# The last feed-forward block's products seven instead of eight, and the table load of attention tied to eight silus

## The chip, the cores and the metric

One NeuronCore of a Trainium2 chip runs the whole program. The metric is the device time of one execution in microseconds; lower is better.

## The reference

Two layers over x of 512 tokens by 1024 features, float32. Each layer is: a half-step SwiGLU block, a mixer, another half-step SwiGLU block, each with an RMS norm before it, and a final RMS norm:

```
x = x + 0.5 * (silu(h @ w_gate) * (h @ w_up)) @ w_down      h = rms_norm(x, gain), hidden width 2816
layer 0 mixer: 4 heads of differential attention (softmax) and 4 heads of stick-breaking attention
layer 1 mixer: gated DeltaNet, 8 heads
out = rms_norm(x, final_norm)
```

Stick-breaking attention needs for each score z the logarithm of a sigmoid, a reverse running sum over the keys and an exponential: for each block of scores an Abs, an Exp, a Ln and one more Exp on ScalarE.

## The kernel before

x lies in SBUF with features on the partitions: eight chunks of 128 features by 512 tokens (`self.x`). All large products are float32 made from two parts, a rounded high part and the rest (`split_to`, L225 and L226 for operands, L173 and L174 for weights in `panel`), and three matmuls each: high by high, high by low, low by high (`mm3`, L180 to L182). The matmuls that carry the work are therefore 128 x 128 by 512 or 256 columns.

A feed-forward block (`ffn`) cuts the 22 tiles of the hidden width into groups. In three of the four blocks the groups have 6, 8 and 8 tiles. The first group's gate and up products are made by `eight`: for a pair of hidden tiles 2 weight matrices x 2 tiles x 8 feature chunks x 3 = 96 matmuls of 512 columns. The other two groups use `seven`: tokens and features are halved and the 2 x 2 block product is formed from seven half-size products with sums and differences of the operands, for a pair 7 x 2 x 4 x 3 = 168 matmuls of 256 columns (L499). The combined x operands are prepared once a block by `quarters`; the combined weights are loaded and partly summed by accumulating DMAs that GpSimd issues (L472), by two sums on VectorE (L513, L525), and split as other weights are. After each group `add_out` multiplies the group's hidden tiles with their rows of w_down and adds the result to x by VectorE (L374).

The fourth block, the last of the program, has groups of 12 and 10 tiles, all by `eight`. After its first group x is turned to tokens on the partitions (`to_tokens`, L546 and L549: 32 transposes, eight copies), and `add_tok` adds both groups' results token-wise. In its last call each 128 tokens' row goes on into `finish`, the final norm: squares on ScalarE, a power on GpSimd, two scalings and one output DMA for 128 tokens by 1024 features (L601). In the last half of the output columns the last three weight panels are multiplied together token block by token block, so that the four blocks end one after the other.

Every activation needs its function in ScalarE's active table. At the start of attention, `exp_ln_tables` (L187) puts in a load of the one set `natural_log_exp_and_others`; an ordering tie to `self.last_act`, the silu issued last in program order, says that it comes after that silu, and attention's first Exp (L626) is tied behind the load. Loads that the program does not name are put in by the build where a function is not in the active set; the profile shows them under the line of the activation they serve.

The order of instructions on each engine is chosen when the program is built, from the program order, data dependencies, buffers and such ties. PSUM tiles come from three rings: `mm_ps` with two buffers, `a_ps` and `b_ps` with three each. In stick-breaking attention (`sb_block`) three blocks of scores are live at once (`W_SB`), two heads by four query blocks a group, and two groups follow each other; the next group's projections and the first part of the output projection are multiplied between them.

Of the kernel before, what the change touches and what calls it, by code (L numbers as in the profile page):

```python
# [10 lines left out]
F32 = mybir.dt.float32  # L11
F32R = mybir.dt.float32r
AF = mybir.ActivationFunctionType
ALU = mybir.AluOpType

P = 128
T = 512
D = 1024
KC = D // P
FF = 2816  # L20
NF = FF // P
NB = T // P
# [78 lines left out]
class Trunk:  # L101
# [4 lines left out]
    def __init__(self, ctx, tc):  # L106
        self.tc = tc
        self.nc = tc.nc
        self.const = ctx.enter_context(tc.tile_pool(name="const", bufs=1))
        self.xp = ctx.enter_context(tc.tile_pool(name="xp", bufs=1))  # L110
        self.wp = ctx.enter_context(tc.tile_pool(name="wp", bufs=4))
        self.np_ = ctx.enter_context(tc.tile_pool(name="np", bufs=2))
        self.ps = ctx.enter_context(tc.tile_pool(name="ps", bufs=2, space=bass.MemoryType.PSUM))
        self.dram = ctx.enter_context(tc.tile_pool(name="dr", bufs=1, space=bass.MemoryType.DRAM))
        self.ahead, self.pending, self.pin = [], [], None
        self.te = self.nc.tensor
        self.x = [self.xp.tile([P, T], F32, name=f"x{c}") for c in range(KC)]
        self.consts()
# [65 lines left out]
    def exp_ln_tables(self):  # L184

        nc = self.nc
        ld = nc.scalar.add_instruction(mybir.InstLoadActFuncSet(  # L187
            name=nc.get_next_instruction_name(), act_func_set_id=EXP_LN_SET, ins=[], outs=[]))
        dep = mybir.DependencyInfo(mybir.DependencyClass.NoSync, mybir.DependencyReason.DATA)
        self.tc.add_manual_dep(ld.ins, self.last_act.ins.name, dep, reason="tables")  # L190
        return ld, dep


# [184 lines left out]
    def ffn(self, wg, wu, wd, first=False, last=None):  # L378

        nc = self.nc
        sizes, ring = ((12, 10), 14) if last is not None else ((6, 8, 8), 10)
        with ExitStack() as st:
            pool = st.enter_context(self.tc.tile_pool(name="ffn", bufs=2))
            f0 = 0
            for size in sizes:
                hid = []
                for f in range(f0, f0 + size, 2):
                    if f0 and last is None:  # L390
                        inner = self.seven(pool, wg, wu, f)
                    else:
                        inner = self.eight(pool, wg, wu, f, first)
                    for j, hd in enumerate(inner):
                        slot = (f + j) % ring
                        both = pool.tile([P, 2 * T], F32R, tag=f"hid{slot}", name=f"hid{slot}",
                                         bufs=1)
                        h, l = both[:, :T], both[:, T:]
                        self.split_to(h, l, hd)
                        hid.append((h, l))  # L400
                if f0 == 0:
                    if last is None:
                        self.quarters(pool)
                    else:
                        self.to_tokens(pool)
                if last is None:
                    self.add_out(hid, wd, f0 * P, 0.5, (self.a_ps, self.a_ps, self.b_ps, self.b_ps))
                else:
                    self.add_tok(hid, wd, f0 * P, 0.5, f0 and self.finish(pool, *last))
                f0 += size  # L410

    def small(self, pool, tag):
# [3 lines left out]
    def eight(self, pool, wg, wu, f, first):  # L416

        nc = self.nc
        g = self.proj_pair(wg, f * P, (self.a_ps, self.b_ps) if f == 2 else None,
                           2 if first and f == 0 else 1)  # L420
        u = self.proj_pair(wu, f * P, (self.a_ps, self.b_ps))
        for j in range(2):
            gr, sg, ur, hd = (self.small(pool, t) for t in ("gr", "sg", "ur", "hd"))
            nc.vector.tensor_tensor(gr, g[j], self.rb, op=ALU.mult)
            self.last_act = nc.scalar.activation(sg, gr, AF.Silu)
            nc.vector.tensor_tensor(ur, u[j], self.rb, op=ALU.mult)
            nc.vector.tensor_tensor(hd, sg, ur, op=ALU.mult)  # L427
            yield hd
# [35 lines left out]
    def seven(self, pool, wg, wu, f):  # L464
# [65 lines left out]
        for lo, hi in ((X, c21), (c12, c22)):  # L530
            sg, hd = self.small(pool, "sg"), self.small(pool, "hd")
            for i, c in enumerate((lo, hi)):
                s = slice(i * 256, (i + 1) * 256)
                self.last_act = nc.scalar.activation(sg[:, s], c[:, :256], AF.Silu)
                nc.vector.tensor_tensor(hd[:, s], sg[:, s], c[:, 256:], op=ALU.mult)
            yield hd

    def to_tokens(self, pool):
        nc = self.nc
        self.xt = []  # L540
        for b in range(NB):
            t = pool.tile([P, D], F32, name=f"xt{b}", bufs=1)
            for hf in range(2):
                ps = self.a_ps()
                for c in range(4):
                    nc.tensor.transpose(out=ps[:, c * P:(c + 1) * P],  # L546
                                        in_=self.x[hf * 4 + c][:, b * P:(b + 1) * P],
                                        identity=self.ident)
                nc.vector.tensor_copy(t[:, hf * 512:(hf + 1) * 512], ps)  # L549
            self.xt.append(t)  # L550

    def add_tok(self, parts, w, row0, factor, after=None):


        nc = self.nc
        n = len(parts)
        for dh in range(2):
            ps = [self.a_ps(), self.a_ps(), self.b_ps(), self.b_ps()]
            starts = list(range(0, n, 2))
            groups = [[f0] for f0 in starts[:-NSPL]] + [starts[-NSPL:]]  # L560
            for group in groups if dh else [[f0] for f0 in starts]:
                ws = [self.panel(w[row0 + f0 * P:row0 + (f0 + 2) * P, dh * 512:(dh + 1) * 512]
                                 .rearrange("(k p) c -> p k c", p=P), 2, 512) for f0 in group]
                for b in range(NB):
                    s = slice(b * P, (b + 1) * P)
                    for f in range(group[0], group[-1] + 2):
                        h, l = ws[(f - group[0]) // 2]
                        ph, pl = parts[f]
                        self.mm3(ps[b], (ph[:, s], pl[:, s]), (h[:, f % 2], l[:, f % 2]),
                                 f == 0, f == n - 1)  # L570
            for b in range(NB):
                xs = self.xt[b][:, dh * 512:(dh + 1) * 512]
                nc.vector.scalar_tensor_tensor(xs, ps[b], factor, xs, ALU.mult, ALU.add)
                if after:
                    after(b, dh)

    def finish(self, pool, gain, out):

        nc = self.nc
        gb = pool.tile([P, D], F32, name="gfin", bufs=1)  # L580
        nc.scalar.dma_start(gb, gain.rearrange("(o d) -> o d", o=1).broadcast_to([P, D]))
        sums = [pool.tile([P, 2], F32, name=f"fss{b}", bufs=1) for b in range(NB)]
        halves = slice(0, T), slice(T, D)

        def step(b, hf):
            x, ss = self.xt[b], sums[b]
            sq = self.np_.tile([P, T], F32, tag="sq", name="sq")
            nc.scalar.activation(sq, x[:, halves[hf]], AF.Square, accum_out=ss[:, hf:hf + 1])
            if hf == 0:
                nc.vector.tensor_scalar(ss[:, 0:1], ss[:, 0:1], 1.0 / D, EPS, ALU.mult, ALU.add)  # L590
                nc.vector.tensor_tensor(x[:, halves[0]], x[:, halves[0]], gb[:, halves[0]],
                                        op=ALU.mult)
                return
            ms = pool.tile([P, 1], F32, tag="fms", name="fms")
            nc.vector.scalar_tensor_tensor(ms, ss[:, 1:2], 1.0 / D, ss[:, 0:1], ALU.mult, ALU.add)
            r = pool.tile([P, 1], F32, tag="fr", name="fr")
            self.rpow(r, ms, 1)
            nc.scalar.activation(x[:, halves[0]], x[:, halves[0]], AF.Copy, scale=r)
            nc.vector.scalar_tensor_tensor(x[:, halves[1]], x[:, halves[1]], r, gb[:, halves[1]],
                                           ALU.mult, ALU.mult)  # L600
            nc.sync.dma_start(out[b * P:(b + 1) * P, :], x)  # L601

        return step

# [724 lines left out]
```

## Time and profile before

| what | value |
|---|---|
| median of 3 runs | 2018.27 us (2018.04 to 2020.41) |
| the profiled execution's own time | 2018.62 us |
| its span, first to last instruction | 2016.9 us |
| VectorE, ScalarE, GpSimd busy | 65%, 44%, 13% of the span |
| mean granted TensorE clock | 0.992 |
| DMA | 230.28 MB, mean 114 GB/s |

The profiled execution is 0.35 us over the median and 1.7 us longer than its own span. PE is TensorE's matmuls, PEld its weight loads, DVE VectorE, ACT ScalarE, POOL GpSimd, SP SyncE. A busy PE is modelled from starts: where matmuls follow closely the count of matmuls in a stretch is the better measure of what one costs.

### The profile page before, as it was taken

How to read it: one execution, taken by the hardware profiler on the slowest of the kernel's cores; microseconds unless marked ns; L12 is line 12 of the kernel's file. 1: busy time of each engine (PE TensorE's matmuls, PEld its weight loads, DVE VectorE, ACT ScalarE, POOL GpSimd, SP SyncE). 2: the span in 40 equal slices, each digit the busy share in tenths (PEclk: the TensorE clock that was granted, in tenths of full speed). 3: DMA queues.
4: the chain of work that ended last, by engine and by line, in shares of the span. 5: the costliest groups of instructions: out<-in, count | busy, mean ns of one | idle time of the engine just before them, and what ended most of it. 6: DMA issues, size and time to landing. Idle time of an engine off the chain costs nothing.

```text
span 2016.9 us, 29447 instructions
## 1 busy us (share of the span) xinstructions
PE 1967.6 (98%) x11514; PEld 1720.1 (85%) x11514; DVE 1304.0 (65%) x2058; ACT 897.3 (44%) x1577; POOL 254.6 (13%) x394
## 2 busy tenths in 40 slices
PE   8999999999899999999999999998899999999998
PEld 7899898888778899998889999876787788888887
DVE  6867485796557776575677667577577575443543
ACT  5434254466874344353334434455455453222322
POOL 1021110100000021110103011005441400000000
PEclk9999999999999999999999999999999999999999
DMA  7568453221135487543648654344333233322331
GB/s 200 151 132 209 92 128 105 88 83 53 47 88 136 127 171 176 114 105 106 156 131 173 167 125 95 106 116 107 80 81 86 72 110 94 95 94 94 97 101 73
DMA packets 291263, 230.28 MB, mean 114 GB/s; under 512 B 31618, under 2 KB 266420, under 8 KB 291124
## 3 DMA queue, kind: packets, MB, share of 16 engines
q1 hardware_dynamic: 209604, 195.21, 31.7%
q0 software_dynamic: 50688, 25.17, 10.2%
q10 hardware_dynamic: 30832, 8.02, 1.7%
q8 instruction: 90, 1.47, 0.3%
q14 instruction: 49, 0.40, 0.1%
HBM read 223.10 MB, written 5.26 MB: 113 GB/s over the span
## 4 chain that ended last, share of the span: by engine, by line
PE 60%; POOL 5%; DMA 2%; DVE 2%; issue 1%; ACT 1%; ACTq 0%; POOLq 0%; DVEq 0%
PE pa L499 7%; PE pa L182 5%; PE pa L180 5%; PE pa L181 5%; PE pb L182 5%; PE pb L180 5%; PE pb L181 5%; PE mm L95 5%; PE pb L499 5%; PE mm L499 5%; PE mm L181 3%; PE mm L182 3%; PE mm L180 3%; POOL tmp L1162 2%; POOL rr L1165 2%
## 5 line engine op out<-in xcount | busy, mean ns | idle before, releaser
L174 DVE TENSOR_TENSOR wl<-raw,wh 128x1024 fp32r<-128x1024 f32 (+1 forms) x252 | 295.4, 1173 | 271.6 <-ACT wh L173 270.7
L173 ACT CAST wh<-raw 128x1024 fp32r<-128x1024 f32 (+1 forms) x252 | 254.4, 1010 | 427.8 <-PE pb L181 153.5
L180 PE MATMUL mm<-xnh,wh 128*128 128x512 f32 (+1 forms) x432 | 168.7, 394 | 7.9 <-DVE qT L663 5.6
L182 PE MATMUL mm<-xnh,wl 128*128 128x512 f32 (+1 forms) x432 | 168.6, 392 | 0.0
L181 PE MATMUL mm<-xnl,wh 128*128 128x512 f32 (+1 forms) x432 | 168.2, 390 | 0.0
L226 DVE TENSOR_TENSOR wl<-raw,wh 128x1024 fp32r<-128x1024 f32 x72 | 88.0, 1223 | 79.0 <-ACT wh L225 79.0
L225 ACT CAST wh<-raw 128x1024 fp32r<-128x1024 f32 x72 | 75.5, 1049 | 113.6 <-PE pb L499 43.9
L95 PE MATMUL mm<-xnh,wh 128*128 128x512 f32 x256 | 109.1, 426 | 12.9 <-DVE cx L1051 12.9
L499 PE MATMUL pa<-sx,wh 128*128 128x256 f32 x576 | 109.9, 283 | 0.0
L180 PEld LDWEIGHTS mm<-xnh,wh 128*128 128x128 f32 x432 | 82.9, 192 | 25.5 <-DVE qT L663 6.6
L181 PE MATMUL pa<-hid,wh 128*128 128x512 f32 x264 | 102.8, 389 | 0.0
L182 PE MATMUL pa<-hid,wl 128*128 128x512 f32 x264 | 102.7, 389 | 0.0
L181 PE MATMUL pb<-hid,wh 128*128 128x512 f32 x264 | 102.7, 389 | 0.0
L182 PE MATMUL pb<-hid,wl 128*128 128x512 f32 x264 | 102.7, 389 | 0.0
L180 PE MATMUL pa<-hid,wh 128*128 128x512 f32 x264 | 102.3, 389 | 0.0
L180 PE MATMUL pb<-hid,wh 128*128 128x512 f32 x264 | 102.2, 389 | 0.0
L472 POOL DMA_DIRECT2D raw<-in_ffn_w_gate_dram x24 | 30.9, 1289 | 561.0 <-DMA raw<-in_ffn_w_gate_dram 306.8
L95 PE MATMUL mm<-xnl,wh 128*128 128x512 f32 x256 | 101.6, 397 | 0.0
L95 PE MATMUL mm<-xnh,wl 128*128 128x512 f32 x256 | 101.5, 396 | 0.0
L182 PEld LDWEIGHTS mm<-xnh,wl 128*128 128x128 f32 x432 | 82.7, 191 | 15.9 <-issue 0.5
L181 PEld LDWEIGHTS mm<-xnl,wh 128*128 128x128 f32 x432 | 82.8, 192 | 15.6 <-issue 0.2
L225 ACT CAST hid<-hd 128x512 fp32r<-128x512 f32 x88 | 54.5, 619 | 81.3 <-DVE hd L427 72.9
(395 smaller groups left out, 5626.8 us busy)
## 6 DMA issues: line engine op xcount, KB each, us to landing
raw<-in_ffn_w_down_dram SPq DMA_DIRECT2D x88, 512.0 KB, 3.7
raw<-in_ffn_w_gate_dram SPq DMA_DIRECT2D x40, 512.0 KB, 3.7
raw<-in_ffn_w_up_dram SPq DMA_DIRECT2D x40, 512.0 KB, 3.6
raw<-in_gdn_w_in_dram SPq DMA_DIRECT2D x32, 512.0 KB, 3.9
sr<-in_ffn_w_gate_dram SPq DMA_DIRECT2D x24, 512.0 KB, 3.8
sr<-in_ffn_w_up_dram SPq DMA_DIRECT2D x24, 512.0 KB, 4.9
raw<-in_att_w_in_dram SPq DMA_DIRECT2D x24, 512.0 KB, 3.6
sb<-in_ffn_w_gate_dram SPq DMA_DIRECT2D x24, 256.0 KB, 3.8
```

The costliest lines, as they stand in the source:

```text
L95: return self.tc.keep_in_program_order(self.engine.matmul(*args, **kw))
L173: nc.scalar.copy(out=h[:, :n], in_=raw[:, :n])
L174: nc.vector.tensor_tensor(l[:, :n], raw[:, :n], h[:, :n].bitcast(F32), op=ALU.subtract)
L180: self.te.matmul(out, lhsT=lh, rhs=rh, start=start, stop=False)
L181: self.te.matmul(out, lhsT=lh, rhs=rl, start=False, stop=False)
L182: self.te.matmul(out, lhsT=ll, rhs=rh, start=False, stop=stop)
L225: nc.scalar.copy(out=h, in_=src)
L226: nc.vector.tensor_tensor(l, src, h.bitcast(F32), op=ALU.subtract)
L472: eng.dma_start(v[:, q * 4:q * 4 + 4], w[kh * 512:(kh + 1) * 512, f * P + lo:f * P + hi] .rearrange("(k p) c -> p k c", p=P), **kw)
L499: nc.tensor.matmul(out, lhsT=wt[:, q * 4 + k], rhs=xt, start=start and q + k + i == 0, stop=q == 1 and k == 3 and i == 2, skip_group_check ...
L1162: nc.gpsimd.tensor_tensor(p, rr[:, :k, j:j + 1].broadcast_to(sh), lb[:, j, j + 1:].rearrange("p (o m) -> p o m", o=1) .broadcast_to(sh), o ...
L1165: nc.gpsimd.tensor_tensor(rr[:, :k, j + 1:], rr[:, :k, j + 1:], p, op=ALU.subtract)
```

## The change

Three edits. The last block gets the groups 6, 8, 8 of the others: the first group by `eight`, the other two by `seven`; `add_out` serves its first two groups, and x is turned to tokens only ahead of the last group, into the buffers of x's own chunks. The final norm uses smaller scratch buffers and writes each 128 tokens in two output DMAs. The table load of attention is tied to the last eight silus in place of one.

```diff
@@ exp_ln_tables
-        self.tc.add_manual_dep(ld.ins, self.last_act.ins.name, dep, reason="tables")
+        for act in self.silus[-8:]:
+            self.tc.add_manual_dep(ld.ins, act.ins.name, dep, reason="tables")
@@ ffn
-        sizes, ring = ((12, 10), 14) if last is not None else ((6, 8, 8), 10)
+        sizes, ring = (6, 8, 8), 10
-                    if f0 and last is None:
+                    if f0:
                         inner = self.seven(pool, wg, wu, f)
                 if f0 == 0:
-                    if last is None:
-                        self.quarters(pool)
-                    else:
-                        self.to_tokens(pool)
-                if last is None:
+                    self.quarters(pool)
+                if last is None or f0 + size < NF:
                     self.add_out(hid, wd, f0 * P, 0.5, (self.a_ps, self.a_ps, self.b_ps, self.b_ps))
                 else:
-                    self.add_tok(hid, wd, f0 * P, 0.5, f0 and self.finish(pool, *last))
+                    self.to_tokens()
+                    self.add_tok(hid, wd, f0 * P, 0.5, self.finish(pool, *last))
@@ eight, seven
-            self.last_act = nc.scalar.activation(sg, gr, AF.Silu)
+            self.silus.append(nc.scalar.activation(sg, gr, AF.Silu))
@@ to_tokens
+        self.xt = [[] for _ in range(NB)]
+        for hf, mk in enumerate(((self.b_ps, self.a_ps), (self.mm_ps, self.a_ps))):
+            ps = [mk[b // 2]() for b in range(NB)]
+            for b in range(NB):
                 for c in range(4):
+                    nc.tensor.transpose(out=ps[b][:, c * P:(c + 1) * P],
                                         in_=self.x[hf * 4 + c][:, b * P:(b + 1) * P],
                                         identity=self.ident)
+            for b in range(NB):
+                c = hf * 4 + b
+                t = self.xp.tile([P, T], F32, tag=f"x{c}", name=f"xt{c}")
+                if b % 2:
+                    nc.scalar.copy(out=t, in_=ps[b])
+                else:
+                    nc.vector.tensor_copy(t, ps[b])
+                self.xt[b].append(t)
@@ add_tok
-            ps = [self.a_ps(), self.a_ps(), self.b_ps(), self.b_ps()]
+            ps = [self.b_ps(), self.b_ps(), self.a_ps(), self.a_ps()]
@@ finish
-        gb = pool.tile([P, D], F32, name="gfin", bufs=1)
+        gb = pool.tile([P, D], F32, tag="sb", name="gfin")
...
-            nc.sync.dma_start(out[b * P:(b + 1) * P, :], x)
+            for t, s in zip(x, halves):
+                nc.sync.dma_start(out[b * P:(b + 1) * P, s], t)
```

## Rows read from the trace of the kernel before

**Rows 1.** The page's first part: busy time and share of the span.

```profile
PE 1967.6 (98%) x11514; PEld 1720.1 (85%) x11514; DVE 1304.0 (65%) x2058; ACT 897.3 (44%) x1577; POOL 254.6 (13%) x394
```

**Rows 2.** Busy by stretch (PE, PEld, DVE, ACT, POOL (count), clock, DMA): feed-forward groups.

```profile
711.30:791.95 80.65, 80.65 (x674) 80.63 (x672) 62.33 (x75) 39.28 (x53) 18.21 (x14) 1.00 0.84 183
...
1183.60:1264.24 80.64, 80.64 (x673) 80.61 (x672) 62.33 (x75) 39.28 (x53) 13.02 (x10) 1.00 0.56 119
1846.41:1955.17 108.76, 108.76 (x481) 90.09 (x480) 50.76 (x59) 32.45 (x39) 0.00 (x0) 1.00 0.34 107
```

**Rows 3.** Busy by stretch, same columns: stick-breaking batches, then differential attention.

```profile
489.00:530.00 41.00, 32.08 (x144) 24.05 (x143) 21.71 (x47) 38.88 (x63) 2.06 (x2) 0.92 0.10 33
549.00:586.00 37.00, 32.09 (x139) 24.73 (x138) 22.97 (x42) 35.22 (x62) 0.00 (x0) 0.91 0.11 36
390.00:440.00 50.00, 50.00 (x319) 45.26 (x318) 46.33 (x110) 30.49 (x74) 0.00 (x0) 1.00 0.24 75
```

**Rows 4.** ScalarE's groups by line, 488 to 592 us: busy, mean ns, idle.

```profile
L816 ACT ACT_TABLE_LOAD x14 | 18.0, 1283 | 0.2
L826 ACT ACT_TABLE_LOAD x9 | 11.5, 1283 | 0.2
...
L815 ACT ACT_TABLE_LOAD x5 | 6.4, 1283 | 0.1
```

**Rows 5.** ScalarE in order of time (start, us, instruction): three short stretches.

```profile
315.74 1.28 ACT L187 ACT_TABLE_LOAD   x1
...
318.09 1.28 ACT L534 ACT_TABLE_LOAD   x1
...
321.64 0.41 ACT L534 ACTIVATE sg<-ur 128x256 f32<-128x256 f32 x1
...
387.82 1.28 ACT L626 ACT_TABLE_LOAD   x1
...
490.73 1.28 ACT L816 ACT_TABLE_LOAD   x1
...
492.24 0.29 ACT L813 ACTIVATE e<-z 128x128 f32<-128x128 f32 x1
492.55 1.28 ACT L815 ACT_TABLE_LOAD   x1
```

**Rows 6.** TensorE's waits, 488 to 592 us: total, times, longest.

```profile
PE mm L180 <- DVE qT L663: 5.6, 1, 5.6
PE pa L832 <- ACT aT L801: 4.1, 3, 2.0
```

**Rows 7.** TensorE by line and shape, 489 to 530 us: count, busy, mean ns.

```profile
L180 PE MATMUL mm<-xnh,wh 128*128 128x512 f32 x30 | 13.8, 459 | 5.8 <-DVE qT L663 5.6
...
L808 PE MATMUL pb<-kT,qT 128*128 128x512 f32 x4 | 2.0, 593 | 0.0
...
L770 PE MATMUL pa<-v,aT 128*128 128x128 f32 x9 | 1.2, 275 | 0.0
```

**Rows 8.** The same view, 549 to 586 us.

```profile
L180 PE MATMUL mm<-xnh,wh 128*128 128x512 f32 x32 | 13.8, 437 | 1.4 <-DVE x L374 1.4
...
L832 PE MATMUL pa<-aT,v 128*128 128x128 f32 x24 | 4.1, 322 | 3.5 <-ACT aT L801 3.5
```

**Rows 9.** The chain that ended last, near 1777 us: start, us, what.

```profile
1777.60 0.87 PE pa L546 x8
```

**Rows 10.** The token tiles: each instruction's count, min/median/max ns, first and last start.

```profile
L549 DVE COPY xt<-pa x8: 678/680/691, 1778.2 to 1789.6; 128x512 f32<-128x512 f32 x8
...
L601 SPq DMA_DIRECT2D out_dram<-xt x4: 332/344/357, 2004.9 to 2013.0; - x4
```

**Rows 11.** The quartered x, same columns.

```profile
L442 DVE SCALAR_TENSOR_TENSOR xr<-x,norms,rb x24: 739/743/748, 42.6 to 991.8; 128x512 f32<-128x512 f32 x24
```

**Rows 12.** VectorE in order of time, end of another block's last seven.

```profile
1264.45 0.69 DVE L505 TENSOR_TENSOR ur<-pb,u 128x512 f32<-128x512 f32 x1 [0.31 <-PE pb L499]
```

**Rows 13.** The gate weights' loads: time from issue to landing.

```profile
DMA to landing us min/median/max: 2.8/4.4/10.0
```

More of the change, by code (lines that the diff above doesn't have):

```diff
@@ L114, in __init__ @@
         self.dram = ctx.enter_context(tc.tile_pool(name="dr", bufs=1, space=bass.MemoryType.DRAM))
-        self.ahead, self.pending, self.pin = [], [], None
+        self.ahead, self.pending, self.pin, self.silus = [], [], None, []
         self.te = self.nc.tensor
@@ L378, in ffn @@
     def ffn(self, wg, wu, wd, first=False, last=None):
-        nc = self.nc
-        sizes, ring = ((12, 10), 14) if last is not None else ((6, 8, 8), 10)
+        sizes, ring = (6, 8, 8), 10
         with ExitStack() as st:
@@ L533, in seven, with to_tokens, add_tok @@
                 s = slice(i * 256, (i + 1) * 256)
-                self.last_act = nc.scalar.activation(sg[:, s], c[:, :256], AF.Silu)
+                self.silus.append(nc.scalar.activation(sg[:, s], c[:, :256], AF.Silu))
                 nc.vector.tensor_tensor(hd[:, s], sg[:, s], c[:, 256:], op=ALU.mult)
             yield hd
-    def to_tokens(self, pool):
+    def to_tokens(self):
         nc = self.nc
[L540 to L544, printed above, removed]
+        self.xt = [[] for _ in range(NB)]
+        for hf, mk in enumerate(((self.b_ps, self.a_ps), (self.mm_ps, self.a_ps))):
+            ps = [mk[b // 2]() for b in range(NB)]
+            for b in range(NB):
                 for c in range(4):
-                    nc.tensor.transpose(out=ps[:, c * P:(c + 1) * P],
+                    nc.tensor.transpose(out=ps[b][:, c * P:(c + 1) * P],
                                         in_=self.x[hf * 4 + c][:, b * P:(b + 1) * P],
                                         identity=self.ident)
-                nc.vector.tensor_copy(t[:, hf * 512:(hf + 1) * 512], ps)
-            self.xt.append(t)
-    def add_tok(self, parts, w, row0, factor, after=None):
+            for b in range(NB):
[6 more added lines that the diff above has]
+                self.xt[b].append(t)
+    def add_tok(self, parts, w, row0, factor, after):
         nc = self.nc
@@ L571, in add_tok @@
             for b in range(NB):
-                xs = self.xt[b][:, dh * 512:(dh + 1) * 512]
+                xs = self.xt[b][dh]
                 nc.vector.scalar_tensor_tensor(xs, ps[b], factor, xs, ALU.mult, ALU.add)
-                if after:
-                    after(b, dh)
+                after(b, dh)
     def finish(self, pool, gain, out):
         nc = self.nc
-        gb = pool.tile([P, D], F32, name="gfin", bufs=1)
+        gb = pool.tile([P, D], F32, tag="sb", name="gfin")
         nc.scalar.dma_start(gb, gain.rearrange("(o d) -> o d", o=1).broadcast_to([P, D]))
-        sums = [pool.tile([P, 2], F32, name=f"fss{b}", bufs=1) for b in range(NB)]
+        sums = pool.tile([P, 2 * NB], F32, name="fss", bufs=1)
@@ L583, in finish @@
         halves = slice(0, T), slice(T, D)
         def step(b, hf):
-            x, ss = self.xt[b], sums[b]
+            x, ss = self.xt[b], sums[:, 2 * b:2 * b + 2]
             sq = self.np_.tile([P, T], F32, tag="sq", name="sq")
-            nc.scalar.activation(sq, x[:, halves[hf]], AF.Square, accum_out=ss[:, hf:hf + 1])
+            nc.scalar.activation(sq, x[hf], AF.Square, accum_out=ss[:, hf:hf + 1])
             if hf == 0:
                 nc.vector.tensor_scalar(ss[:, 0:1], ss[:, 0:1], 1.0 / D, EPS, ALU.mult, ALU.add)
-                nc.vector.tensor_tensor(x[:, halves[0]], x[:, halves[0]], gb[:, halves[0]],
-                                        op=ALU.mult)
+                nc.vector.tensor_tensor(x[0], x[0], gb[:, halves[0]], op=ALU.mult)
@@ L593, in step @@
                 return
-            ms = pool.tile([P, 1], F32, tag="fms", name="fms")
+            ms = self.np_.tile([P, NB], F32, tag="ms", name="fms")[:, :1]
             nc.vector.scalar_tensor_tensor(ms, ss[:, 1:2], 1.0 / D, ss[:, 0:1], ALU.mult, ALU.add)
-            r = pool.tile([P, 1], F32, tag="fr", name="fr")
+            r = self.np_.tile([P, NB], F32, tag="rt", name="fr")[:, :1]
             self.rpow(r, ms, 1)
-            nc.scalar.activation(x[:, halves[0]], x[:, halves[0]], AF.Copy, scale=r)
@@ L599, in step @@
-            nc.vector.scalar_tensor_tensor(x[:, halves[1]], x[:, halves[1]], r, gb[:, halves[1]],
-                                           ALU.mult, ALU.mult)
-            nc.sync.dma_start(out[b * P:(b + 1) * P, :], x)
+            nc.scalar.activation(x[0], x[0], AF.Copy, scale=r)
+            nc.vector.scalar_tensor_tensor(x[1], x[1], r, gb[:, halves[1]], ALU.mult, ALU.mult)
+            for t, s in zip(x, halves):
+                nc.sync.dma_start(out[b * P:(b + 1) * P, s], t)
         return step
```

## The prediction

> **What bounds the kernel now.** I read the page's shares first: TensorE is busy 98% of the span, VectorE 65%, ScalarE 44% [rows 1]. So only two things shorten this program: fewer or cheaper matmuls, or a stretch in which TensorE stands still. The busy times by stretch show both. In the feed-forward blocks TensorE is full: a group of four pairs by seven products has 672 matmuls of 256 columns in 80.64 us, and the last block's five pairs by eight have 480 of 512 columns in 108.76 us [rows 2] (the counts shown are one or two higher, by matmuls that overlap the edges). That is 0.1200 and 0.2266 us a matmul. In stick-breaking attention it is not full: in two stretches of 41 and 37 us it is busy 32.1 us each at a granted clock of 0.92 and 0.91, while ScalarE is busy 38.9 and 35.2 us, that is 95% [rows 3]. ScalarE's groups by line say with what: 28 table loads of 1.283 us, 35.9 us [rows 4].
>
> **Why there are loads.** In order of time, the named load stands at 315.74, but silus follow it, the last at 321.64; the first of them has its own load at 318.09, which undoes the named one [rows 5]. Attention's first Exp then loads again at 387.82, and from 490.73 on Exp and Ln alternate, each with a load. The Abs at 492.24 has none. So a load comes only where the active set lacks the function, and after a lost combined set the two functions are served from two sets.
>
> **Part 1, the tie.** The silu tied to was not the last on the engine. Eight silus are those of the last two pairs, four each, and the earlier ones lie 40 us back, so the load now falls behind 321.64. The tie orders one engine and adds no semaphore. Behind the load ScalarE has weight casts, and it is busy only 39.3 of 80.6 us in such a stretch [rows 2], so its 1.28 us cost nothing there; the loads at 318.09 and 387.82 go, also worth nothing. If Exp and Ln then share one set, the 28 loads go, and that is what counts.
>
> The Trainium skill (ScalarE: Activation LUTs, "Table sets: the hidden batching unit") lists natural_log_exp_and_others as holding both exp and ln; by that none of the 28 would be left, and without it all would stay. No row here shows Exp and Ln running under that set.
>
> What this is worth is not 35.9 us but what TensorE has to spare. Its work in the first stretch: 89 matmuls of 512 columns (the first of their three lines stands in [rows 7]) at 0.2266 are 20.2 us; 41 transposes and products of 128 columns (the last of four lines) at 0.109, from eight in 0.87 us [rows 9], are 4.5; 14 score matmuls, which I put at no more than 0.2266, 3.2. Sum 27.9 of 41 us. The second stretch has 92, 36 and 11 [rows 8]: 20.8 + 3.9 + 2.5 = 27.2 of 37. So 55.1 of 78 us are work and **22.9 us** could go: the upper end. ScalarE would be left with 74.1 - 35.9 = 38.2 us, VectorE has 44.7, both below 55. The listed waits of TensorE are behind ScalarE's queue: 4.1 us on its copies and 5.6 us on a VectorE instruction [rows 6] that itself stands behind one waiting for a Ln. The lower clock goes with the idle time that it follows. What is late next is VectorE. For the lower end I let it be filled no better than its mean share of 65% [rows 1]: 44.7 / 0.65 = 69 us, a gain of 9. But in differential attention, with the same kind of chains, it is busy 46.33 of 50 us and TensorE never idles [rows 3]. That is the nearest row, so I take 20 and leave 2.9 us for the ends of the two batches.
>
> **Part 2, seven in the last block.** Eight pairs change: eight products cost 108.76 / 5 = 21.75 us a pair, seven 80.64 / 4 = 20.16 [rows 2]. 8 x 1.59 = **12.7 us**. The two groups shown agree within 0.01 us, so as long as the block runs as the others do this is firm, 12 to 13; a stall is a rival below. What comes with it: `quarters` puts eight scalings of 0.743 us [rows 11] and, at 0.68 us as in [rows 10], some 22 sums and splits on VectorE, 21 us, beside the first group's output product, 144 x 0.2266 = 32.6 us. Of DMAs, a pair has eight issues on SP and four on POOL in place of four on SP; POOL is busy 13 of 81 us with them in the other blocks and DMA engines 56% [rows 2], with nothing of TensorE lost. The output product costs the same in either form: 24 matmuls for a hidden tile. Were this cover gone, each pair's weights would show, as in the last rival.
>
> The Trainium skill (TensorE: Matmul & The Clock Gate, "Wait — 56ns, not 53.3ns?") gives columns over 2.4 GHz plus some 2.5 ns for every matmul: 109 and 216 ns. As an estimate by it the part is worth 8 x (96 x 0.2158 - 168 x 0.1092) = 19.0 us. The measured 120 ns is above it, so the sum goes by the rows.
>
> **Part 3, tokens at the end.** The 32 transposes, 3.5 us by [rows 9], only move: from the middle, between matmuls, to the last products' end. There `add_tok` wants first the `b_ps` buffer of the last seventh product, which comes free with a combination of 0.69 us that ends 0.8 us after that product [rows 12]; the transposes are work for TensorE in that time, if their buffers are free. The eight copies, 0.68 us on VectorE [rows 10], are halved between it and ScalarE: 2.7 us each, beside 5.4 us of the first weight panel's products. The final norm's gain is loaded on ScalarE's queue into a buffer that the next-to-last pair has left some 20 us earlier, so the casts behind it don't wait. I take 0.3 us, between 0 and the 6 of a rival.
>
> **Part 4, the output.** Eight issues instead of four, 0.344 us each on SP [rows 10]. Only the last pair of them is at the end: the second goes out up to 0.35 us later, with half the bytes: -0.3 to +0.7, I take 0.2.
>
> **Sum**, against the profiled execution's own 2018.62 us: -20.0 - 12.7 + 0.3 + 0.2 = -32.2, so 1986.4. That execution is 0.35 us over the median of the runs: **1986.1 us**.
>
> **Rivals.**
> - *VectorE takes ScalarE's place* in the two batches, or their dependencies do: gain 9 instead of 20, **1997**. For it: scans and sums of a block follow each other strictly. Against: the differential stretch.
> - *The tie doesn't do it*: a silu still lands behind the load, or the build gives Exp its own set again. The loads stay, only parts 2 to 4 count: **2006**. Against: all four silus of a pair are now tied, and the Abs without a load says that membership decides.
> - *The turn to tokens stands open*: transposes and copies in a row, 3.5 + 2.7 us with nothing beside them: **1992**.
> - *Seven products cost half columns*: in the seven stretches the weight load is busy 80.6 of 80.6 us, in the eight one 90 of 109 [rows 2]; so 256 columns cost 0.120 and not half of 0.2266. Were the load not in the way, 8 x (21.75 - 168 x 0.1133) = 21.7 us: **1977**. The skill's rule above is of this kind; six groups in three blocks speak against it.
> - *Slower*: the last block's sevens starve for weights. The gate weights' loads land in 4.4 us in the median, 10.0 at worst [rows 13]; if each of the eight pairs waited for the difference, 8 x 5.6 = 45 us and the time is **2031**. It decides from 32.2 / 8 = 4.0 us a pair. Against: three blocks do the same without a wait.
>
> **How the numbers follow.** Forecast 0.70, VectorE 0.12, tie 0.06, turn 0.05, half columns 0.02, slower 0.03, and 0.02 for times near the old one that I don't see. The range takes the forecast with its upper end (22.9 instead of 20, and a little for the open ends of parts 3 and 4: 1982, less 2), and the VectorE and turn cases: 1980 to 1998. No change means within 0.2%, about what a measurement of this kernel can tell. All cases but the last two are faster by more: 0.95, 0.02, 0.03.
>
> **What would show it.** In the profile after: one load at about 322 and none between 488 and 592; the two batches shorter by 20 us together, at clock 1.00, ScalarE well under 95%. In the last block two stretches of 672 matmuls in 80.6 us each; no TensorE gap over 1 us between the last of them and the first output product. Wrong would be: loads under the lines of Exp and Ln; TensorE waits on VectorE in the batches; idle time before products of the last block.

## The result, and the profile after

The changed kernel takes 1985.26 us (median of 4 runs, 1984.48 to 1986.73) beside 2018.79 us (2018.04 to 2020.41) for the kernel before: a ratio of 0.983, with an interval of 0.982 to 0.985. The forecast was 1986.1, in a range from 1980 to 1998. The profiled execution took 1985.88 us, with a span of 1984.1 us.

The page's first part answers to [rows 1]. The columns are busy time, share of the span and instructions:

```profile
PE 1950.0 (98%) x12090; PEld 1735.8 (87%) x12090; DVE 1376.1 (69%) x2156; ACT 897.6 (45%) x1613; POOL 296.4 (15%) x426
```

ScalarE's busy time over the whole span is as before, although 35.9 us of table loads went, because the last block now gives it 38.1 us more to do (below): the page's totals hide that trade, and only views of single stretches show it. These are, in the changed kernel, stretches inside the two stick-breaking batches (columns as in [rows 2], answering to [rows 3]):

```profile
484.00:526.00 42.00, 42.00 (x251) 36.08 (x250) 27.64 (x54) 26.85 (x65) 2.11 (x2) 1.00 0.17 55
535.00:570.00 35.00, 35.00 (x181) 28.71 (x179) 26.09 (x46) 23.46 (x57) 0.00 (x0) 1.00 0.17 53
```

TensorE is full, at the full clock. ScalarE is at 64 and 67%, VectorE at 66 and 75%. For the worth of it, one stretch is taken from the last silu of the feed-forward block to the table load that opens the next block, first in the kernel before, then in the changed one:

```profile
321.64:637.99 316.35, 301.88 (x1628) 257.10 (x1627) 210.13 (x425) 190.62 (x364) 17.03 (x17) 0.98 0.29 85
```

```profile
320.63:615.58 294.95, 294.95 (x1629) 254.56 (x1628) 210.36 (x425) 155.15 (x335) 17.09 (x17) 1.00 0.31 91
```

The stretch is 21.4 us shorter. TensorE's count and VectorE's time are the same to a hair, and ScalarE is busy 35.5 us less, with 29 instructions fewer. The 21.4 us have two parts: TensorE's idle time, 316.35 - 301.88 = 14.5 us, went, and its busy time for the same matmuls fell by 6.9 us, since the granted clock of the stretch rose from 0.98 to 1.00.

Why ScalarE has less to do stands in its timeline (start, us, instruction), which answers to [rows 5]:

```profile
320.63 0.41 ACT L532 ACTIVATE sg<-ur 128x256 f32<-128x256 f32 x1
321.06 1.28 ACT L187 ACT_TABLE_LOAD   x1
322.44 0.62 ACT L226 CAST hid<-hd 128x512 fp32r<-128x512 f32 x1
...
615.58 1.28 ACT L423 ACT_TABLE_LOAD   x1 [9.12 <-DVE gr L422]
```

The named load stands right behind the last silu, and no other comes until the next block's silus. By lines, from 300 to 600 us, ScalarE has one group of loads, where [rows 4] has 28 loads:

```profile
L187 ACT ACT_TABLE_LOAD x1 | 1.3, 1283 | 0.0
```

The last block as a whole, from the end of the gated DeltaNet stage to the end of the span, and the changed kernel's two groups of seven products in it. First before, then after:

```profile
1634.20:2016.90 382.70, 375.54 (x1676) 310.88 (x1674) 179.85 (x229) 114.70 (x149) 3.19 (x5) 1.00 0.30 98
```

```profile
1612.40:1984.10 371.70, 363.21 (x2252) 327.91 (x2250) 251.33 (x327) 152.81 (x215) 44.76 (x37) 0.99 0.55 135
...
1725.20:1805.80 80.60, 80.60 (x673) 80.60 (x672) 62.34 (x75) 39.27 (x53) 18.11 (x14) 1.00 0.83 184
1849.35:1930.00 80.65, 80.65 (x674) 80.63 (x673) 61.70 (x74) 39.28 (x53) 12.94 (x10) 1.00 0.57 125
```

The groups take what [rows 2] show for the other blocks, with TensorE never idle, and the block is 11.0 us shorter: TensorE's busy time fell by 12.3 us, its idle time in the block grew by 1.3, from 7.16 to 8.49 us. Between 1640 and 1985 us, one wait of TensorE is over 1 us (engine, tile and line, what it waited for: total, times, longest):

```profile
PE pa L182 <- DVE wl L174: 1.6, 1, 1.6
```

It stands in the first group's gate and up products (the tile `xnh` is the normed x), 31 us ahead of the block's first output product, which starts at 1692.54. TensorE's row, and VectorE's timeline, which says why:

```profile
1661.59 0.50 PE L182 MATMUL pa<-xnh,wl 128*128 128x512 f32 x1 [1.59 <-DVE wl L174]
...
1653.82 5.38 DVE L440 SCALAR_TENSOR_TENSOR xr<-x,norms,rb 128x512 f32<-128x512 f32 x8
1659.12 0.68 DVE L425 TENSOR_TENSOR hd<-sg,ur 128x512 f32<-128x512 f32 x1
1659.72 0.68 DVE L424 TENSOR_TENSOR ur<-pb,rb 128x512 f32<-128x512 f32 x1
1660.32 2.35 DVE L174 TENSOR_TENSOR wl<-raw,wh 128x1024 fp32r<-128x1024 f32 x2
```

The eight scalings that quarter x run in one piece right behind the block's norm, and the split of the weight that the matmul at 1661.59 wants stands behind them.

The turn to tokens, in TensorE's timeline at the end of the last seven products:

```profile
1930.63 0.28 PE L497 MATMUL pb<-sx,wl 128*128 128x256 f32 x1
1930.75 0.27 PE L544 MATMUL pb<-ident,x 128*128 128x128 f32 x1
1930.86 1.04 PE L544 MATMUL pa<-ident,x 128*128 128x128 f32 x8
1931.73 1.04 PE L544 MATMUL mm<-ident,x 128*128 128x128 f32 x8
1932.60 0.60 PE L544 MATMUL pa<-ident,x 128*128 128x128 f32 x4
1932.96 0.48 PE L180 MATMUL pb<-wh,hid 128*128 128x512 f32 x1
```

Transposes follow the last product with no gap, and the output product follows them with none.

### The profile page after: what moved, and what is told of

It is laid out like the page before. It is cut to its first block, busy times and chain, and to the rows that moved or that the text cites. A ratio compares the mean times of both kernels' runs of the same rounds, so it can differ in the third digit from the quotient of the medians.

```text
span 1984.1 us, 30930 instructions
## 1 busy us (share of the span) xinstructions
PE 1950.0 (98%) x12090; PEld 1735.8 (87%) x12090; DVE 1376.1 (69%) x2156; ACT 897.6 (45%) x1613; POOL 296.4 (15%) x426
## 3 DMA queue, kind: packets, MB, share of 16 engines
q1 hardware_dynamic: 227076, 199.41, 32.8%
q0 software_dynamic: 67584, 33.56, 13.8%
## 4 chain that ended last, share of the span: by engine, by line
PE 87%; POOL 5%; DVE 2%; DMA 2%; issue 1%; ACT 1%; ACTq 0%; SPq 0%; POOLq 0%; DVEq 0%
PE pa L497 14%; PE pb L497 9%; PE mm L497 9%; PE pb L182 6%; PE pb L180 6%; PE pb L181 6%; PE pa L182 5%; PE pa L180 5%; PE pa L181 5%; PE mm L95 4%; PE mm L180 4%; PE mm L182 4%; PE mm L181 4%; POOL tmp L1164 2%; POOL rr L1167 2%
## 5 line engine op out<-in xcount | busy, mean ns | idle before, releaser
L181 PE MATMUL pa<-hid,wh 128*128 128x512 f32 x320 | 124.6, 389 | 0.0
L180 PE MATMUL pa<-hid,wh 128*128 128x512 f32 x320 | 123.9, 389 | 0.0
L497 PEld LDWEIGHTS pa<-sx,wh 128*128 128x128 f32 x768 | 119.8, 192 | 0.0
L180 PE MATMUL mm<-xnh,wh 128*128 128x512 f32 (+1 forms) x304 | 117.0, 389 | 0.7 <-ACT wh L173 0.6
L182 PE MATMUL mm<-xnh,wl 128*128 128x512 f32 (+1 forms) x304 | 117.4, 388 | 0.0
L181 PE MATMUL mm<-xnl,wh 128*128 128x512 f32 (+1 forms) x304 | 116.9, 386 | 0.0
L497 PE MATMUL pa<-xnh,wh 128*128 128x256 f32 x384 | 108.8, 283 | 0.0
L497 PE MATMUL mm<-xnh,wl 128*128 128x256 f32 x384 | 108.7, 283 | 0.0
L497 PE MATMUL pa<-sx,wl 128*128 128x256 f32 x384 | 108.7, 283 | 0.0
L497 PE MATMUL pa<-xnh,wl 128*128 128x256 f32 x384 | 108.7, 283 | 0.0
L497 PE MATMUL mm<-xnl,wh 128*128 128x256 f32 x384 | 108.7, 283 | 0.0
```

The costliest lines, as they stand in the source:

```text
L180: self.te.matmul(out, lhsT=lh, rhs=rh, start=start, stop=False)
L181: self.te.matmul(out, lhsT=lh, rhs=rl, start=False, stop=False)
L182: self.te.matmul(out, lhsT=ll, rhs=rh, start=False, stop=stop)
L497: nc.tensor.matmul(out, lhsT=wt[:, q * 4 + k], rhs=xt, start=start and q + k + i == 0, stop=q == 1 and k == 3 and i == 2, skip_group_check ...
```

## The experiments

Each is timed beside the kernel before, on the same chip as it, except the fifth, which is a single execution. Differences from one kernel to another go by those medians and by the traces. In this section "the changed kernel" is the one above; run again word for word (the tenth), its median was 1986.55 us instead of 1985.26, so a difference of 1 or 2 us between kernels timed apart from each other is not shown by the medians.

**One part each.** The first puts the tie alone into the kernel before:

```diff
-        self.tc.add_manual_dep(ld.ins, self.last_act.ins.name, dep, reason="tables")
+        for act in self.silus[-8:]:
+            self.tc.add_manual_dep(ld.ins, act.ins.name, dep, reason="tables")
```

> The kernel before with the tie to eight silus and nothing else. Theory (the 28 table loads in the stick-breaking batches go, and TensorE fills what it had to spare): 1997 us, 21 to 22 us under the kernel before; one load near 321 us and none between 487 and 570 us, TensorE without idle time there. Rival (the gain of the whole change lies in the last block, or one part needs the other): within 4 us of the kernel before, or a gain clearly other than 22 us.

Measured: 1997.86 us (1996.95 to 1998.46), a ratio of 0.990 [0.988, 0.991]. The second is the changed kernel with the load tied to one silu, as before:

```diff
-        for act in self.silus[-8:]:
+        for act in self.silus[-1:]:
```

> The changed kernel with the tie to the last silu alone, as before the change. Theory (the parts add): 2007 us, 11 us under the kernel before; 28 loads back in the two batches, the last block as in the changed kernel with two stretches of 672 matmuls in 80.6 us each. Rival (VectorE or the weights limit the last block): over 2010 us.

Measured: 2006.99 us (2006.36 to 2009.32), 0.994 [0.993, 0.996]. Against the 2019.3 us of the kernel before on that chip, the tie alone gives 21.4 us and the rest alone 12.3. Together that is 33.7 us; the whole change gave 33.5. Each of these is known to about 3 us by its interval; within that the parts add up, so neither takes anything from the other that would show, and the rival by which the tie does nothing is out.

**Loads or order.** A tie moves an instruction, and the gain could come from its place. The third experiment leaves each instruction of the changed kernel where it is and names another set, which holds Exp and not Ln:

```diff
-EXP_LN_SET = list(get_activation_tables("trn2")).index("natural_log_exp_and_others")
+EXP_LN_SET = list(get_activation_tables("trn2")).index("exp_and_others")
```

> The changed kernel with the tie to eight silus kept, but the table that the named load brings is the set of exp without ln; everything else, the order of ScalarE's other instructions too, as in the changed kernel. Theory (the loads are what costs, not where the named load stands or what order came with it): 2006 to 2008 us, 21 to 22 us over the changed kernel. Rival (the place of the load and the order that follows from it brought the gain): within 4 us of the changed kernel.

Measured: 2008.26 us (2007.44 to 2009.5), 0.995 [0.993, 0.996]. ScalarE's groups of loads in the two batches are back:

```profile
L818 ACT ACT_TABLE_LOAD x14 | 18.0, 1283 | 0.2
L828 ACT ACT_TABLE_LOAD x9 | 11.5, 1283 | 0.2
L817 ACT ACT_TABLE_LOAD x5 | 6.4, 1283 | 0.1
```

and stretches in the batches look as they did before the change, with the lower clock too:

```profile
488.30:529.30 41.00, 33.19 (x138) 25.21 (x137) 22.38 (x47) 38.88 (x65) 2.06 (x2) 0.88 0.11 33
548.30:585.30 37.00, 31.41 (x139) 23.60 (x138) 22.41 (x39) 34.68 (x61) 0.00 (x0) 0.95 0.12 36
```

The load at the same place, of a set without Ln, brings back all 28 loads and 23.0 us, although the other instructions of TensorE, VectorE, ScalarE and GpSimd stand in the same order as in the changed kernel's trace. What the tie is worth is the loads and nothing of the order.

**What a load costs.** If the loads cost what ScalarE lacks and not their own length, some of them should be nearly free. The fourth experiment adds, to the changed kernel, a load of the same set ahead of each Exp in the two batches, 16 in all:

```diff
-        nc.scalar.activation(e[:, :n], z[:, :n], AF.Abs)
+        ab = nc.scalar.activation(e[:, :n], z[:, :n], AF.Abs)
         yield
-        nc.scalar.activation(e[:, :n], e[:, :n], AF.Exp, scale=-1.0)
+        ld = nc.scalar.add_instruction(mybir.InstLoadActFuncSet(...))
...
+        self.tc.add_manual_dep(ld.ins, ab.ins.name, dep, reason="tables")
+        ex = nc.scalar.activation(e[:, :n], e[:, :n], AF.Exp, scale=-1.0)
+        self.tc.add_manual_dep(ex.ins, ld.ins.name, dep, reason="tables")
```

> The changed kernel with one more load of the same set in each of the 16 blocks of stick-breaking attention, 20.5 us of ScalarE. Theory (loads cost only what they go beyond ScalarE's spare time beside TensorE, some 27 us in the two batches): 0 to 4 us over the changed kernel, TensorE still busy over 95% of the batches. Rival (every load lies on the chain of a block, so time goes with their number): 16/28 of 22 us, 12 us over the changed kernel.

Measured: 1990.64 us (1987.69 to 1990.93), 0.986 [0.984, 0.987]. That is 5.4 us over the changed kernel in the medians, somewhat more than my theory gave and half of the proportional one. The stretch from the last silu to the next block's load is 2.9 us longer (322.06 to 619.86), so about half of the 5.4 us lies in it; another 1.4 us lie ahead of it (322.06 against 320.63), where nothing was changed. Two stretches inside the batches show ScalarE taking up the loads:

```profile
488.00:530.00 42.00, 42.00 (x251) 36.16 (x251) 28.99 (x57) 37.02 (x73) 1.98 (x2) 1.00 0.16 51
538.00:575.00 37.00, 36.62 (x176) 29.53 (x175) 24.85 (x43) 30.19 (x57) 0.00 (x0) 1.00 0.19 58
```

With 20.5 us more of work ScalarE is busy 37 of 42 us, and TensorE is still full in the first stretch and idle for 0.4 us in the second. The order of ScalarE's instructions also shifted around the added loads, so the 5.4 us are not the loads alone. As a rough reading, since the 16 stand in other places than the 28: 16 loads cost 3 to 5 us, 28 cost 21, so the last dozen costs 16 to 18, more than their own 12 x 1.28 = 15.4. So a load is cheap while ScalarE has room. With ScalarE busy 88% in the first stretch here, TensorE never stood still and kept the full clock; with 95% before the change it stood still for 8.9 of 41 us, and the granted clock was 0.92 [rows 3].

**What makes 256 columns dear.** The prediction said that the weight load stands in the way of the sevens' matmuls. The fifth experiment halves their columns and keeps every weight load; it leaves out half of those products' arithmetic, in all blocks:

```diff
+            cut = lambda t, i: t[:, i % 2 * 128:i % 2 * 128 + 128]
...
-                        nc.tensor.matmul(out, lhsT=wt[:, q * 4 + k], rhs=xt,
+                        nc.tensor.matmul(cut(out, i), lhsT=wt[:, q * 4 + k], rhs=cut(xt, i),
```

> The changed kernel with every matmul of the seven products cut to 128 of its 256 columns (high and low parts write alternating halves), in all four blocks: half of the products' arithmetic is left out. It measures what sets the 0.120 us of such a matmul. If the weight load sets it: start to start stays at 0.11 to 0.12 us, the eight stretches of 672 matmuls stay at 74 to 81 us and the time falls by no more than 55 us. If the columns set it: 0.06 to 0.07 us, each stretch 40 to 47 us unless other engines hold it, and the time falls by well over 150 us, or to where VectorE's 62 us a stretch hold it, some 140 us.

Measured: 1941.05 us in one execution. The seven groups of an earlier block and of the last one:

```profile
678.00:752.95 74.95, 74.95 (x673) 74.95 (x672) 61.57 (x75) 39.23 (x53) 18.20 (x14) 1.00 0.91 193
1691.60:1766.55 74.95, 74.95 (x673) 74.94 (x672) 61.55 (x75) 39.25 (x53) 18.15 (x14) 1.00 0.89 193
```

672 matmuls of 128 columns take 74.95 us, 0.1115 us each, and the time fell by 44 us: what I had written down for the weight load. But that expectation put 0.11 and 0.12 us together, and they differ. A matmul of 256 columns takes 0.1200 and one of 512 takes 0.2266 [rows 2]. So 256 columns more cost 106.6 ns, which is 2.4 columns a ns, one for each tick of the full clock of 2.4 GHz; by that some 13 ns of each matmul, at 256 as at 512, are not columns. On the same line 128 columns would take 67 ns, and they take 111.5: here something other than columns sets the time. With a new weight for every matmul the load is the nearest candidate, but this run keeps every load and can't show it. At 256 columns this floor is not what binds, since 0.1200 is 8.5 ns above it. Half-size products are dear there because a matmul of half the columns pays the 13 ns for half the work. What the 13 ns are, and whether they too come from the new weight, no run here shows.

**Where the turn belongs.** In the sixth experiment x turns to tokens after the first group, as before the change, within the new structure:

```diff
-                if last is None or f0 + size < NF:
+                if f0 == 0 or last is None:
                     self.add_out(hid, wd, f0 * P, 0.5, (self.a_ps, self.a_ps, self.b_ps, self.b_ps))
+                    if last is not None:
+                        self.to_tokens()
                 else:
-                    self.to_tokens()
-                    self.add_tok(hid, wd, f0 * P, 0.5, self.finish(pool, *last))
+                    self.add_tok(hid, wd, f0 * P, 0.5,
+                                 self.finish(pool, *last) if f0 + size == NF else None)
```

> The changed kernel with x turned to tokens after the first group, as before the change, and the second group's product added token-wise too. Theory (the turn at the end is hidden: its transposes fill the time of the last combination and only move): within 1 us of the changed kernel. Rival (the turn stands open at the end): 2 to 6 us faster than the changed kernel.

Measured: 1989.77 us (1987.6 to 1990.82), 0.985 [0.984, 0.987], 4.5 us over the changed kernel in the medians and 2.6 us in the last block of the profiled execution (374.3 against 371.7). I had both places within 1 us; that was wrong. TensorE's waits in the last block:

```profile
PE pa L182 <- DVE wl L174: 1.6, 1, 1.6
PE mm L499 <- ACT p L510: 1.4, 1, 1.4
PE pa L499 <- DVE u L520: 0.8, 1, 0.8
```

The first is the changed kernel's own. The other two, 2.2 us, are of products of seven behind a copy on ScalarE and a sum on VectorE. The longer one ends here, some 8 us after the turn's last transposes at 1730.11:

```profile
1737.97 0.39 PE L499 MATMUL mm<-xnh,wh 128*128 128x256 f32 x1 [1.38 <-ACT p L510]
```

That the turn's own copies hold up these two engines fits, but no run takes them away alone. Within this structure late is the better place for the turn.

**The scalings.** The seventh experiment holds the eight scalings back, in the last block, until the weight split ahead of them is issued:

```diff
-        nc.vector.tensor_tensor(l[:, :n], raw[:, :n], h[:, :n].bitcast(F32), op=ALU.subtract)
+        self.cutw = nc.vector.tensor_tensor(l[:, :n], raw[:, :n], h[:, :n].bitcast(F32), op=ALU.subtract)
...
-                    self.quarters(pool)
+                    with self.tc.issue_after(self.cutw.ins) if last else nullcontext():
+                        self.quarters(pool)
```

> The changed kernel with the quartering of x in the last block held back behind the split of the weight panel last issued before it, so behind the first group's weight splits. Theory (the 1.6 us that the last block misses are TensorE's wait at 1660 us for a weight split behind eight quarter scalings on VectorE): 1.6 us faster, no such wait, and the first seven product still not late. Rival (the quarters are then late for the first seven product): a wait of 2 us or more at the head of the second group and no gain.

Measured: 1984.7 us (1983.31 to 1986.35), 0.983 [0.982, 0.984]. VectorE now does the split right behind a product's scaling, no wait of TensorE is left there, and the last block takes 369.5 us instead of 371.7:

```profile
1656.68 0.69 DVE L425 TENSOR_TENSOR ur<-pb,rb 128x512 f32<-128x512 f32 x1
1657.28 1.22 DVE L174 TENSOR_TENSOR wl<-raw,wh 128x1024 fp32r<-128x1024 f32 x1
...
1614.70:1984.20 369.50, 362.60 (x2252) 328.04 (x2250) 250.85 (x326) 153.07 (x215) 44.87 (x37) 1.00 0.56 136
```

So the place of the scalings causes the wait. In the medians only 0.6 us are left of the gain, which is within what repeats of a kernel differ by: the gated DeltaNet stage ahead of the block, which this edit doesn't touch, was 0.9 us longer in the profiled execution.

**A better version.** Eight products are dearer than seven, and each block does its first group by eight. The eighth experiment makes that group smaller, 4 hidden tiles instead of 6:

```diff
-        sizes, ring = (6, 8, 8), 10
+        sizes, ring = (4, 8, 10), 10
```

> The changed kernel with groups of 4, 8 and 10 tiles in all four blocks, so that one more pair in each goes by seven products. Theory (a pair by seven saves 1.6 us of TensorE and the quartering, 21 us on VectorE, still fits beside the first group's output product of 22 us): 4 x 1.6 = 6.4 us faster, 1979 us. Rival (the shorter first group no longer covers the quartering): waits at the head of the second group, 2 us or more a block, no gain or a loss.

Measured: 1983.98 us (1983.08 to 1984.5), 0.983 [0.981, 0.984], 5 us short of the theory. The four blocks are shorter by 1.6, 1.1, 1.3 and 0.7 us, 4.7 together. TensorE has no wait at the head of a second group, so the rival is out; in the last block the wait of 1.6 us is gone, and one of 2.2 us stands ahead of the first output product, for which the profile names no cause:

```profile
PE pa L180 <- issue: 2.2, 1, 2.2
```

The ninth keeps the old sizes in the last block and adds the seventh's edit there:

```diff
-        sizes, ring = (6, 8, 8), 10
+        sizes, ring = (6, 8, 8) if last else (4, 8, 10), 10
```

> The changed kernel with two edits: groups of 4, 8 and 10 in the first three blocks, and in the last block the quartering held back behind the first group's weight splits, with its groups 6, 8, 8. Theory (each edit's gain in its own blocks adds: 1.6, 1.1 and 1.3 us in the first three blocks, 2.2 us in the last, as the traces of the two single edits show them): 6 us under the changed kernel in the same job, 1979 us. Rival (what the blocks gain is lost in the gated DeltaNet stage, whose length differs by up to 4 us from run to run): within 2 us of the changed kernel.

Measured: 1984.58 us (1982.92 to 1984.96), 0.983 [0.981, 0.984]. The tenth is the changed kernel once more, word for word, in the ninth's company:

> The changed kernel once more, word for word, beside the kernel that joins two edits. It shows how far two jobs and two profiles of one program differ: 1984 to 1987 us, and the same 80.6 us for every stretch of 672 matmuls; the gated DeltaNet stage may differ by 1 to 3 us.

Measured: 1986.55 us (1986.04 to 1988.82), 0.984 [0.983, 0.986]. So the ninth is 2.0 us faster than the changed kernel beside it, with no run of the one as slow as any of the other, and that is a third of what I expected. The eighth has the lowest median of the kernels that do all the arithmetic, by 0.6 us; these two can't be told apart. The gated DeltaNet stage, which the sizes don't touch, gave back 2.7 of the 4.7 us that the blocks gained in the eighth, and 2.2 of 5.2 us in the ninth, as the ninth's rival had it. Its rows in the changed kernel, the same kernel again, the eighth and the ninth:

```profile
1285.40:1612.40 327.00, 306.83 (x1925) 253.71 (x1924) 231.51 (x545) 171.42 (x494) 111.04 (x272) 0.97 0.32 86
```

```profile
1284.70:1611.20 326.50, 303.93 (x1926) 251.12 (x1925) 231.07 (x545) 171.66 (x494) 111.47 (x272) 0.98 0.33 87
```

```profile
1281.40:1611.10 329.70, 308.29 (x1925) 254.81 (x1924) 230.74 (x545) 171.04 (x494) 111.91 (x272) 0.96 0.32 86
```

```profile
1281.70:1610.90 329.20, 308.97 (x1926) 255.48 (x1925) 231.15 (x545) 171.13 (x494) 112.46 (x272) 0.96 0.33 86
```

The work is the same; the longer stages have the lower granted clock. It falls at one place more with the new sizes. In both their traces TensorE waits there for a copy by ScalarE, 1.70 us in the eighth and 1.33 in the ninth, and the granted clock is then 0.50 (1.2 GHz). In the other ten traces the same matmul waits 0.24 us at most, and the clock stays at 1.00. The eighth's wait and a stretch behind it, then the same stretch in the changed kernel, where it comes 4 us later:

```profile
1498.66 1.21 PE L98 MATMUL pa<-ident,on 128*128 128x128 f32 x4 [1.70 <-ACT on L1260]
...
1502.00:1504.00 2.00, 2.00 (x6) 1.59 (x6) 1.87 (x4) 1.28 (x2) 0.00 (x0) 0.50 0.51 107
```

```profile
1506.00:1508.00 2.00, 2.00 (x14) 1.72 (x13) 2.00 (x4) 1.14 (x2) 0.00 (x0) 1.00 0.60 204
```

The mean clock of the whole program fits: 0.992 or 0.993 in all nine executions with the new sizes, 0.994 or 0.995 in all nine of the changed kernel. So the loss goes with the new sizes. Why ScalarE's copy comes later with them, no run shows.

## Why the prediction was right

**The tie: 20 forecast, 21.4 measured**, where the prediction gave TensorE 22.9 us to spare. The mechanism was right step by step: the load falls behind the last silu, the set lasts through the attention, the 28 loads go, and TensorE fills up with its clock. That membership in the active set decides was read from an Abs without a load [rows 5], and the third experiment shows it. The Trainium skill (ScalarE: Activation LUTs, "Table sets: the hidden batching unit") lists a combined set with exp and ln; the trace agrees, with no load between 322.3 and 615.6 us. That the size came out so close is in part luck. The sum put a score matmul at no more than 0.2266 us. One of 512 columns is busy 0.59 us [rows 7], and in the changed kernel two together take 1.02, so the second starts 0.43 us behind the first:

```profile
498.43 1.02 PE L810 MATMUL pb<-kT,qT 128*128 128x512 f32 x2
```

Read in the same way, those of 384, 256 and 128 columns take 0.32, 0.22 and 0.11 us. With these the score matmuls of the two stretches are 7.8 us instead of 5.7, and by the same sum TensorE had 20.8 us to spare, not 22.9. The change took all of that and 0.6 us more, as much as TensorE stood still outside the two stretches (14.5 us from the last silu to the next block's load, 13.8 of them in the two). The 2.9 us that I left for the ends of the batches weren't needed, and made up for the term that was too small.

**VectorE in ScalarE's place** was the rival with the most weight. It was busy 27.6 of 42 and 26.1 of 35 us, and TensorE never waited there, nor anywhere in the 294.95 us from the last silu to the next block's load: its chains have the slack that the differential stretch promised.

**Seven products: 12.7 forecast, 11.0 measured for the whole block.** The products are as priced, 80.60 and 80.65 us for 672. (GpSimd and the DMA engines were put at 13 of 81 us and 56%; in the first of the two groups they were busier, 18.11 us and 83%, as a row of [rows 2] already had it, with nothing of TensorE lost.) The failed step is the cover of `quarters`, which I put "beside the first group's output product": the scalings ran 33 us ahead of it, behind the norm and beside the group's gate and up products, and held up a weight split for 1.6 us. With 1.6 added, the 11.0 are 12.6, of which 0.3 is the shorter end below; the other 12.3 are TensorE's busy time. The seventh experiment takes the wait away by the place of the scalings alone. The price of an edit hidden by another engine's work depends on where the scheduler puts it, and I took it to be where the code calls it.

**Half columns** was rightly put low, by six groups that agreed, but its reading of the weight load was not shown. PEld at 80.6 of 80.6 us [rows 2] looked as if the weight load bound the sevens; the fifth experiment sends the same loads through in 74.95 us, so a busy PEld was no sign of that. At 256 columns the columns and some 13 ns make up the 0.1200 us. The Trainium skill (TensorE: Matmul & The Clock Gate, "Wait — 56ns, not 53.3ns?") states some 2.5 ns a matmul over its columns; here it is 13, at both sizes.

**The turn: 0.3 forecast, none measured.** No wait shows in the timeline above, so the rival in which it stands open (6 us) is out. The sixth experiment's 2.6 us say that beside sevens the late place is the better one, which I had not seen.

**The output: +0.2 forecast, -0.3 measured.** From the start of the last matmul to the end of the span it was 2009.35 to 2016.9, 7.5 us, and is now 1976.86 to 1984.1, 7.2 us. The eight issues of half the bytes land in 2.2 us in the median:

```profile
L603 SPq DMA_DIRECT2D out_dram<-xt x8: 332/344/423, 1972.5 to 1980.8; - x8
...
DMA to landing us min/median/max: 2.0/2.2/2.3
```

The sum by the traces is -21.4 - 11.0 = -32.4, the turn and the output being inside the block's 11.0, against the forecast's -32.2: the tie's 1.4 us more and the wait's 1.6 us less cancel by chance. The span itself fell by 32.8 us. **The slower rival**, starved weights, needed 4 us a pair; the only wait over 1 us in the whole block is the 1.6 us.

## What to carry to other kernels

When a busy engine alternates between two functions with a table load each time, look at what undid the common set, and tie its load to everything that could run behind it on that engine, not to what the program wrote last. Price such loads by what the bounding engine has to spare in that stretch, its idle time and the clock it loses with it, and not by their sum: sixteen loads put where ScalarE had room cost 3 to 5 us of their 20.5, all 28 cost 21 of 35.9. When a gain in one stage doesn't reach the total, compare the waits and the granted clock of the stages that were not touched. And where an added piece is "covered", check which instruction of the covering engine's queue it will stand in front of.

## What was not expected of the hardware

A fp32r matmul (these are the products made from two parts) of 128 columns with a new weight each time takes 0.1115 us, hardly less than one of 256 columns (0.1200), while 512 take 0.2266. A score matmul of plain float32 and 512 columns takes 0.43. And the gated DeltaNet stage, with the same work in all kernels of this study, takes 325.4 us (the second experiment) to 329.7 us (the eighth) at a granted clock between 0.96 and 0.98. The two traces with the new group sizes are the longest, 329.2 and 329.7 us, and have the lowest clock; the other ten lie between 325.4 and 328.2 us, and what sets one of these apart from another stays open. That is as large as the last microseconds that one would want to tune for here.
